# Opening stage of a two-layer decoder trunk: remainders moved from GpSimd to VectorE, and to an accumulating DMA for the last three steps

## The chip, the cores and the metric

One core of one Trainium2 chip runs the kernel. The metric is the device time of one execution in microseconds (us); less is better. Before the change the median of three runs is 1287.88 us (1286.55 to 1293.02).

## What is computed

Two layers over 512 rows of 1024 channels (`x`), conditioned on one vector `c`:

```python
c_act = silu(c)
for l in range(2):
    sh1, sc1, g1, sh2, sc2, g2 = split(c_act @ w_ada[l] + b_ada[l], 6)
    h = rmsnorm(x, norm1_w[l]) * (1 + sc1) + sh1
    x = x + g1 * hybrid_mixer(h, cos, sin, w_in[l], ...)     # attention and state-space heads
    h = rmsnorm(x, norm2_w[l]) * (1 + sc2) + sh2
    x = x + g2 * swiglu(h, w_gate_up[l], w_down[l])
```

`cos` and `sin` are of `positions * inv_freq`. What matters here is the very beginning of layer 0: the norm of `x`, the two modulation vectors `sc1` and `sh1`, the hidden `h`, and the first 808 columns of `h @ w_in[0]`.

## The kernel before, in words

Every f32 product is done as three matmuls in a rounded type (fp32r): an operand is split into a high part (`hi`, `hh`: the rounded copy, made on ScalarE) and a remainder (`lo`, `hl`: the operand minus its high part). The product is hi·hh + hi·hl + lo·hh (`mm3`, line 316; `mmrow`, line 321). So each weight tile costs a DMA, a cast on ScalarE and a subtraction on VectorE or GpSimd.

The stage that changes is the block at lines 1088 to 1156, called the opening below. In the trace it ends where the first `wps` matmul begins, which belongs to the next stage.

- `xin` is loaded transposed into `xT` (channels on partitions), in two halves of the rows, four DMAs each (line 231). `cb` is `c` on all partitions; `silu` is applied to it.
- `stat` (line 1102) makes the squares on ScalarE, adds them up on VectorE, and sums them over the channels by matmuls with `ones`. `scale` (line 1111) turns the sum into the row scale `rs0`, with a logarithm and an exponential on ScalarE and three operations on VectorE.
- Then come eight steps, k = 0 to 7, one for each 128 channels. `load(k)` (line 1114) fetches two tiles of `w_ada` (`raws`, 512 KB each; one for `sc1`, tile 8 + k, one for `sh1`, tile k) and one slab of `w_in` (`rawk`, 404 KB). A tile of `w_ada` is multiplied by `cb` and summed on VectorE (`ada1`, line 332, the result goes into `mods`); `ada_fin` (line 347) adds the bias, and makes `gn` = (1 + sc1) · norm weight. `slab` (line 295) casts `rawk` to `hik` on ScalarE and subtracts to get `lok` on GpSimd (line 300).
- `hid` (line 422) makes the hidden of those 128 channels: `ht` on VectorE (needs `gn`), `hh` on ScalarE (adds `sh1`), a second ScalarE pass `hu`, and `hl` = `hu` - `hh` on GpSimd (line 433).
- `mms` (line 1120) issues the step's 21 matmuls: 12 with 424 columns and 9 with 512.
- In step 2 (`PLAN['STK']`) the small tables are made (`small_tables`, line 252): 25 small VectorE operations on 64 columns for the rotary angles (`ang`, `kk`, `kh`, `kl`), three sines on ScalarE with a table load before them and another after them, and casts of the mask on GpSimd.

All loads go through one queue (SP), in program order. The order of the other engines is set by a scheduler at build time, except where `kept` or `pinned` holds the written order (lines 1129 to 1141). `warm` issues matmuls on `ones` that compute nothing. Buffers that tie the steps together: six for `raws`, three each for the slab and for its high part and remainder.

Of the kernel before, what the change touches and what calls it, by code (L numbers as in the profile page):

```python
# [8 lines left out]
F32 = mybir.dt.float32  # L9
# [3 lines left out]
AF = mybir.ActivationFunctionType  # L13
# [58 lines left out]
    'KHV': 0,  # L72
# [3 lines left out]
P = 128  # L76
S = 512
# [68 lines left out]
class Kept:  # L146
    """an engine; while kept, its instructions stay in the order they are written in"""
# [19 lines left out]
class Stream:  # L167
    """steps for the tensor engine; a step yields the time from which on the next should find its data"""
# [26 lines left out]
def trunk(ctx, tc, xin, cin, pos, eye, consts, small, wada, ws, out):  # L195
# [39 lines left out]
    tc.keep_in_program_order(nc.scalar.preload_act_table_set("silu_and_others"))  # L235
    nc.sync.dma_start(cb, cin.partition_broadcast(P))
    xload(HALVES[0])
    xload(HALVES[1])
    nc.sync.dma_start(sm[0], small[0])
# [12 lines left out]
    def small_tables():  # L252
        ve.tensor_copy(idb, ident)
        mk = kc[:, K_MASK:K_MASK + P]
        for i in range(4):
            tc.keep_in_program_order(ge.tensor_copy(mkb[:, i, :], mk))
# [3 lines left out]
        ang, kk, kh, kl = (tiny(nm, n, 1) for nm in ("ang", "kk", "kh", "kl"))  # L260
# [19 lines left out]
        ve.tensor_scalar(ang, ang, pi, -pi, op0=ALU.min, op1=ALU.max)  # L280
        v4 = lambda t: t.rearrange("p (c f) -> p c f", f=16)
# [3 lines left out]
        ve.tensor_copy(cs2[:, :, 1, :], cs2[:, :, 0, :])  # L285

# [8 lines left out]
    def slab(raw, src, name, n, eng=None):  # L295
        r2, hi, lo = (t.rearrange("p a b -> p (a b)")[:, 0:n] for t in (
            raw, wp.tile([P, 8, P], F32R, name=f"hi{name}", tag="hi"), wp.tile([P, 8, P], F32R, name=f"lo{name}", tag="lo")))
        nc.sync.dma_start(r2, src[:, 0:n])
        se.copy(hi, r2)
        (eng or ve).tensor_tensor(lo, r2, hi.bitcast(F32), op=ALU.subtract)  # L300
        return hi, lo
# [19 lines left out]
    def mmrow(ps, h, w, k, c):  # L321
        """one k of the latents of chunk c, rows on the partitions"""
# [46 lines left out]
    def rsqrt(y, x, scale, name, a=None, out=None):  # L369
        """y = (x * scale + EPS) ** -0.5: exp(-ln / 2) and a Newton step"""  # L370
# [13 lines left out]
    class Norm:  # L384
        """adaLN over the columns of xT: squares added up tile by tile, then the row scale and the hidden"""
# [16 lines left out]
        def scale(self, sl, ps=None, rb=None):  # L402
            """(mean square + eps) ** -0.5 of the rows in sl, on all partitions"""
# [55 lines left out]
    def mixer(l, h, rows, first):  # L459
        s_ = sm[l]  # L460
        with tc.tile_pool(name=f"mx{l}", bufs=1) as mp:
# [14 lines left out]
            def decays():  # L476
                """time steps and decays, [step in chunk, (chunk, head)]"""
# [40 lines left out]
            def dense():  # L518
                """the rest of W_in, then the first half of the rows of W_out, tile by tile"""
# [56 lines left out]
            with tc.tile_pool(name=f"up{l}", bufs=2) as up, psum(f"u{l}", mm=2, ms=2, at=4):  # L576
# [3 lines left out]
                # latents, a chunk's rows on the partitions (their row scale follows after the up-projections)  # L580
# [33 lines left out]
                # rotary factors with the norm weights in them  # L614
# [7 lines left out]
                def rope(x, cw, sw, shape, name, re=ve):  # L622
                    """in place on x[..., 32]"""
# [109 lines left out]
            with tc.tile_pool(name=f"s2{l}", bufs=2) as sp, psum(f"v{l}", ms=2, sc=2, pt=1, op=1, mm=2):  # L733
# [12 lines left out]
                # attention over (chunk, heads), in three steps  # L746
# [34 lines left out]
                def values(c, h0, g):  # L781
                    """two heads at a time, one in each half of the columns of the array: channels on the partitions"""
# [39 lines left out]
                def norms():  # L822
                    """one over the sums of the probabilities, turned to where the channels are; then the products' split"""
# [19 lines left out]
                # the state space part, chunk by chunk  # L843
# [148 lines left out]
    def out_proj(l, mix, nrm, sl, kept):  # L992
        """one half of the rows; the weight tiles that lie on chip at its end are kept for the other half"""
# [93 lines left out]
    for l in range(L):  # L1087
        if l == 0:
            with tc.tile_pool(name="s0", bufs=6) as s0, psum("s", ms=1, st=NCH + NC0):
# [12 lines left out]
                def stat(sl):  # L1102
                    sq = s0.tile([P, KT, S // 2], F32, name=f"sq01{sl.start}", tag="sq", bufs=2)
                    for k in range(0, KT, 2):
                        se.activation(sq[:, k:k + 2], xT[:, k:k + 2, sl], AF.Square)
                        if k > 0:
                            ve.tensor_tensor(sq[:, 0:2], sq[:, 0:2], sq[:, k:k + 2], op=ALU.add)
                    for j in range(2):
                        te.matmul((nst if sl.start else sps[-2])[:, 0:S // 2], ones, sq[:, j], start=j == 0, stop=j == 1)
# [3 lines left out]

                def load(k):
                    for t in (8 + k, k):
                        ada1(0, t, s0.tile([P, 8, P], F32, name=f"raws{t}", tag="raws"))
                        ada_fin(0, t, t + 1)
                    return slab(wraw(f"k{k}"), wk0[k], f"k{k}", NS0, ge)
# [11 lines left out]
                te.pinned = True  # L1130
                warm(PLAN['WU'])
                se.activation(cb, cb, AF.Silu)
                stat(HALVES[0])
                exp_ln_tables()
                warm(PLAN['WV'])
                scale(HALVES[0])
                stat(HALVES[1])
                scale(HALVES[1])
                warm(PLAN['WW'])
                te.pinned = False  # L1140
                ve.kept = se.kept = False
# [151 lines left out]
```

## Time and profile before

| | |
|---|---|
| median of three runs | 1287.88 us |
| lowest, highest run | 1286.55, 1293.02 us |
| span of the profiled execution | 1284.9 us |
| PE busy | 1211.4 us (94%) |
| VectorE (DVE) busy | 634.1 us (49%) |
| ScalarE (ACT) busy | 519.9 us (40%) |
| GpSimd (POOL) busy | 531.1 us (41%) |
| DMA moved | 162.34 MB |

The profiled execution is known by its span alone, from its first instruction to its last; no separate time is listed for it. PE is the matmul engine, PEld its weight loads, SP the DMA queue. Times in rows are us from the start of the span. "Busy" of an instruction runs from its start to its end, so an instruction that is held up by another engine looks long.

### The profile page before, as it was taken

The numbers are of one execution on the slowest core, as the hardware profiler recorded it, in microseconds if no ns is written. First come the engines' busy times: TensorE is split into PE (matmuls) and PEld (weight loads), VectorE is DVE, ScalarE is ACT, GpSimd is POOL, SyncE is SP. The second block draws the span as 40 slices with busy tenths as digits, with TensorE's granted clock in tenths as the row PEclk, the third lists the DMA queues.
The fourth block names the chain that finished last, engine by engine and source line by source line (L and its number), as shares of the span: only waits on it lengthen the run. The fifth ranks groups of instructions, "written<-read, shape, count | busy, mean of one in ns | idle before, by whom it ended". The sixth has DMA issues, their size and how long they took to land. (4 is left out here: it accounts for less than half of the span.)

```text
span 1284.9 us, 16463 instructions
## 1 busy us (share of the span) xinstructions
PE 1211.4 (94%) x6343; PEld 1005.1 (78%) x6344; DVE 634.1 (49%) x1128; ACT 519.9 (40%) x896; POOL 531.1 (41%) x310
## 2 busy tenths in 40 slices
PE   6889796889999999999998999979999999999998
PEld 6768674689888888888887887659988888888888
DVE  6979778879245545211128885576821111110100
ACT  4366774435322222222226668654532222222110
POOL 2651145263676666523333232346333333333231
PEclk9899898899999999999999899999999999999999
DMA  9433352464477777423223222103333332323331
GB/s 321 154 125 102 114 164 99 150 200 143 129 241 238 239 240 237 134 87 97 96 71 107 83 79 70 34 33 91 124 115 99 90 106 84 102 94 107 115 101 40
DMA packets 47855, 162.34 MB, mean 126 GB/s; under 512 B 5344, under 2 KB 8224, under 8 KB 47776
## 3 DMA queue, kind: packets, MB, share of 16 engines
q1 hardware_dynamic: 47776, 161.29, 38.8%
q8 instruction: 50, 0.82, 0.3%
q14 instruction: 29, 0.24, 0.1%
HBM read 159.14 MB, written 2.13 MB: 126 GB/s over the span
## 5 line engine op out<-in xcount | busy, mean ns | idle before, releaser
L292 POOL TENSOR_TENSOR lo<-raw,hi 128x1024 fp32r<-128x1024 f32 x108 | 272.6, 2524 | 338.6 <-ACT hi L156 338.5
L156 ACT CAST hi<-raw 128x1024 fp32r<-128x1024 f32 x179 | 188.0, 1051 | 500.8 <-issue 183.5
L140 PE MATMUL gup<-hl,hi 128*128 128x512 f32 (+1 forms) x736 | 280.4, 381 | 0.0
L140 PE MATMUL gup<-hh,lo 128*128 128x512 f32 (+1 forms) x736 | 279.9, 381 | 0.0
L140 PE MATMUL gup<-hh,hi 128*128 128x512 f32 (+1 forms) x736 | 278.6, 381 | 0.0
L156 DVE TENSOR_TENSOR lo<-raw,hi 128x1024 fp32r<-128x1024 f32 x71 | 88.9, 1253 | 152.6 <-ACT hi L156 150.8
L140 PEld LDWEIGHTS gup<-hh,lo 128*128 128x128 f32 x736 | 139.1, 189 | 26.5
L140 PEld LDWEIGHTS gup<-hl,hi 128*128 128x128 f32 x736 | 139.0, 189 | 26.0 <-DVE hl L156 0.2
L140 PEld LDWEIGHTS gup<-hh,hi 128*128 128x128 f32 x736 | 138.4, 189 | 26.2
L156 DVE SCALAR_TENSOR_TENSOR rawa<-rawa,cb 128x1024 f32<-128x1024 f32 x77 | 111.0, 1443 | 76.7 <-DMA rawa<-wada 76.5
L140 PE MATMUL dps<-ah,hi 128*128 128x512 f32 x308 | 121.8, 396 | 0.0
L140 PE MATMUL dps<-al,hi 128*128 128x512 f32 x308 | 121.8, 396 | 0.0
L140 PE MATMUL dps<-ah,lo 128*128 128x512 f32 x308 | 121.8, 396 | 0.0
L156 DVE TENSOR_TENSOR sg<-sg,gup 128x512 f32<-128x512 f32 x44 | 30.3, 688 | 179.6 <-PE gup L140 173.5
L440 POOL TENSOR_TENSOR al<-sg,ah 128x512 fp32r<-128x512 f32 x44 | 67.6, 1535 | 97.2 <-ACT ah L156 93.6
L140 PE MATMUL ops<-hh,hi 128*128 128x256 f32 x256 | 74.4, 290 | 3.1 <-ACT hi L156 1.5
L140 PE MATMUL ops<-hl,hi 128*128 128x256 f32 x256 | 72.5, 283 | 1.0 <-POOL hl L440 1.0
L140 PE MATMUL wps<-hh,hi 128*128 128x512 f32 x168 | 70.8, 422 | 2.4 <-DVE xbc L156 2.4
L140 PE MATMUL ops<-hh,lo 128*128 128x256 f32 x256 | 72.5, 283 | 0.3 <-POOL lo L292 0.3
L140 PEld LDWEIGHTS dps<-al,hi 128*128 128x128 f32 x308 | 57.9, 188 | 14.1
L140 PEld LDWEIGHTS dps<-ah,hi 128*128 128x128 f32 x308 | 57.9, 188 | 14.0
L140 PEld LDWEIGHTS dps<-ah,lo 128*128 128x128 f32 x308 | 57.9, 188 | 13.9
(303 smaller groups left out, 2103.3 us busy)
## 6 DMA issues: line engine op xcount, KB each, us to landing
raw<-ws SPq DMA_DIRECT2D x181, 512.0 KB, 3.5
rawa<-wada SPq DMA_DIRECT2D x80, 512.0 KB, 4.4
raws<-wada SPq DMA_DIRECT2D x16, 512.0 KB, 5.3
ar<-ard SPq DMA_DIRECT2D x8, 512.0 KB, 3.9
rawk<-ws SPq DMA_DIRECT2D x8, 404.0 KB, 5.4
xT<-xin SPq DMA_DIRECT2D x8, 256.0 KB, 5.9
out<-xT SPq DMA_DIRECT2D x7, 256.0 KB, 2.6
rawr<-ws SPq DMA_DIRECT2D x4, 424.0 KB, 3.2
```

The source lines that it names most:

```text
L140: self._put(self.tc.nc.tensor.matmul(out, lhsT, rhs, **kw), 4 * n if rhs.dtype == F32 else n)
L156: i = f(*args, **kw)
L292: (eng or ve).tensor_tensor(lo[:, :n], raw[:, :n], hi[:, :n].bitcast(F32), op=ALU.subtract)
L440: (eng or ve).tensor_tensor(lo, src, hi.bitcast(F32), op=ALU.subtract)
```

## The change

Ten lines of the plan and of comments aside, the diff does this:

- Two small loads (`posi`, and the frequencies of `kc`) go first on the SP queue, then the first half of `x`, `cb`, `sm`, the second half. The rest of `kc` and `eye` are loaded in step 1.
- The rotary angles are computed at the very start, the sines between the squares and the statistics.
- The squares are no longer added on VectorE: PE sums all eight tiles of a half. Two of the four squares of the second half are made on VectorE.
- The bias and the `1 +` of `gn` are folded into one vector `gb` beforehand, so that `gn` takes one operation.
- `hl` is made on VectorE from `ht`, `sh1` and `hh` in one operation; `hu` is gone.
- `lok` is made on VectorE for k = 0 to 4. For k = 5 to 7 ScalarE writes minus the high part into `lok`, and a DMA issued from GpSimd adds the weights to it from memory.
- Step 0 issues its matmuls by halves of the rows; the second group of warming matmuls stands after both scales, the third is gone.

```diff
     tc.keep_in_program_order(nc.scalar.preload_act_table_set("silu_and_others"))
+    nc.sync.dma_start(posi, pos)
+    nc.sync.dma_start(kc[:, K_FREQ:NK], consts[:, K_FREQ:NK])
+    xload(HALVES[0])
     nc.sync.dma_start(cb, cin.partition_broadcast(P))
-    xload(HALVES[0])
+    nc.sync.dma_start(sm[0], small[0])
     xload(HALVES[1])
-    nc.sync.dma_start(sm[0], small[0])
...
         nc.sync.dma_start(r2, src[:, 0:n])
         se.copy(hi, r2)
+        if eng == "dma":
+            se.activation(lo, r2, AF.Identity, scale=-1.0)
+            ge.dma_start(lo, src[:, 0:n], accum_op=ALU.add)
+            return hi, lo
         (eng or ve).tensor_tensor(lo, r2, hi.bitcast(F32), op=ALU.subtract)
...
-                def stat(sl):
+                def squares(sl):
                     sq = s0.tile([P, KT, S // 2], F32, name=f"sq01{sl.start}", tag="sq", bufs=2)
                     for k in range(0, KT, 2):
-                        se.activation(sq[:, k:k + 2], xT[:, k:k + 2, sl], AF.Square)
-                        if k > 0:
-                            ve.tensor_tensor(sq[:, 0:2], sq[:, 0:2], sq[:, k:k + 2], op=ALU.add)
-                    for j in range(2):
-                        te.matmul((nst if sl.start else sps[-2])[:, 0:S // 2], ones, sq[:, j], start=j == 0, stop=j == 1)
+                        x = xT[:, k:k + 2, sl]
+                        if sl.start and k > 2:
+                            ve.tensor_tensor(sq[:, k:k + 2], x, x, op=ALU.mult)
+                        else:
+                            se.activation(sq[:, k:k + 2], x, AF.Square)
+                    return sq
+
+                def stat(sl, sq):
+                    for k in range(KT):
+                        te.matmul((nst if sl.start else sps[-2])[:, 0:S // 2], ones, sq[:, k], start=k == 0, stop=k == KT - 1)
...
+                nw1 = sm[0][:, C_N1:C_N1 + 8]
+                gb = s0.tile([P, 8], F32, name="gb", bufs=1)
                 def load(k):
                     for t in (8 + k, k):
                         ada1(0, t, s0.tile([P, 8, P], F32, name=f"raws{t}", tag="raws"))
-                        ada_fin(0, t, t + 1)
-                    return slab(wraw(f"k{k}"), wk0[k], f"k{k}", NS0, ge)
+                        m = mods[0][:, t:t + 1]
+                        if t < 8:
+                            ve.tensor_tensor(m, m, sm[0][:, C_BADA + t:C_BADA + t + 1], op=ALU.add)
+                        else:
+                            ve.scalar_tensor_tensor(gn[0][:, k:k + 1], m, nw1[:, k:k + 1], gb[:, k:k + 1], op0=ALU.mult, op1=ALU.add)
+                    return slab(wraw(f"k{k}"), wk0[k], f"k{k}", NS0, "dma" if k > 4 else None)
...
+                angles()
                 warm(PLAN['WU'])
+                sq = squares(HALVES[0])
                 se.activation(cb, cb, AF.Silu)
-                stat(HALVES[0])
+                stat(HALVES[0], sq)
+                sq = squares(HALVES[1])
+                sines()
                 exp_ln_tables()
+                ve.scalar_tensor_tensor(gb, sm[0][:, C_BADA + 8:C_BADA + 16], 1.0, nw1, op0=ALU.add, op1=ALU.mult)
+                stat(HALVES[1], sq)
+                scale(HALVES[0])
+                scale(HALVES[1])
                 warm(PLAN['WV'])
-                scale(HALVES[0])
-                stat(HALVES[1])
-                scale(HALVES[1])
-                warm(PLAN['WW'])
...
                     if k == 1:
+                        nc.sync.dma_start(kc[:, 0:K_FREQ], consts[:, 0:K_FREQ])
                         nc.sync.dma_start(ki, eye)
-                        nc.sync.dma_start(posi, pos)
-                        nc.sync.dma_start(kc, consts)
                     w = load(k)
                     for sl in HALVES if k == 0 else (FULL,):
-                        last = hid(0, 1, h, k, rs0[:, sl], sl, ge)
-                    for sl in HALVES if k < PLAN['KHV'] else (FULL,):
+                        last = hid(0, 1, h, k, rs0[:, sl], sl)
                         mms(k, w, sl)
                     if k == PLAN['STK']:
                         with tc.issue_after(last.ins):
-                            small_tables()
-                        exp_ln_tables()
+                            ve.tensor_copy(idb, ident)
+                            se.copy(cs2[:, :, 1, :], cs2[:, :, 0, :])
+                            for i in range(4):
+                                tc.keep_in_program_order(ge.tensor_copy(mkb[:, i, :], kc[:, K_MASK:K_MASK + P]))
```

`angles()` and `sines()` are the two halves of `small_tables` with the same operations; `ang` and `kh` become tiles that live through the kernel.

## Rows read from the trace of the kernel before

**Rows 1.** Busy time by stretch: us, PE, PEld, DVE, ACT, POOL, clock, DMA share, GB/s.

```profile
200.00:645.00 445.00, 423.58 (x2160) 352.12 (x2160) 219.47 (x336) 149.62 (x222) 226.02 (x117) 0.98 0.51 167
```

**Rows 2.** Timeline of PE: start us, us, operation; the opening's first matmul, step 4's and 5's, the next stage's.

```profile
21.78 0.44 PE L140 MATMUL st<-hik,hh 128*128 128x424 f32 x1
...
55.19 0.35 PE L140 MATMUL st<-hik,hh 128*128 128x424 f32 x1
...
59.62 0.36 PE L140 MATMUL st<-hik,hh 128*128 128x424 f32 x1
...
77.64 0.40 PE L140 MATMUL wps<-hh,hi 128*128 128x512 f32 x1
```

**Rows 3.** PE's waits in the opening: us in total, times, longest us.

```profile
PE st L140 <- POOL hl L433: 7.0, 6, 2.0
```

**Rows 4.** Busy time by stretch, from VectorE's first `raws` to its last `mods`.

```profile
14.99:70.57 55.58, 44.31 (x192) 36.62 (x192) 54.25 (x96) 20.11 (x31) 32.58 (x24) 0.88 0.59 207
```

**Rows 5.** Timeline of VectorE: one `ht` of step 1, then steps 5 and 6, then the last.

```profile
28.13 0.74 DVE L156 SCALAR_TENSOR_TENSOR ht<-xT,gn,rs 128x512 f32<-128x512 f32 x1
...
53.18 1.63 DVE L156 SCALAR_TENSOR_TENSOR ht<-xT,gn,rs 128x512 f32<-128x512 f32 x1
54.73 2.94 DVE L156 SCALAR_TENSOR_TENSOR raws<-raws,cb 128x1024 f32<-128x1024 f32 x1
...
59.53 1.63 DVE L156 SCALAR_TENSOR_TENSOR ht<-xT,gn,rs 128x512 f32<-128x512 f32 x1
...
70.41 0.16 DVE L156 TENSOR_TENSOR mods<-mods,sm 128x1 f32<-128x1 f32 x1
```

**Rows 6.** Timeline of GpSimd over the same steps, and its last `hl`.

```profile
52.98 1.28 POOL L433 TENSOR_TENSOR hl<-hu,hh 128x512 fp32r<-128x512 f32 x1 [1.46 <-ACT hu L156]
54.22 2.37 POOL L300 TENSOR_TENSOR lok<-rawk,hik 128x808 fp32r<-128x808 f32 x1
...
72.02 1.26 POOL L433 TENSOR_TENSOR hl<-hu,hh 128x512 fp32r<-128x512 f32 x1 [2.73 <-ACT hu L156]
```

**Rows 7.** VectorE by line and form, 14.9 to 70.6 us: busy us, mean ns, idle before.

```profile
L156 DVE SCALAR_TENSOR_TENSOR raws<-raws,cb 128x1024 f32<-128x1024 f32 x16 | 26.4, 1650 | 0.0
L156 DVE TENSOR_TENSOR mods<-mods,sm 128x1 f32<-128x1 f32 x16 | 9.5, 594 | 0.2
L156 DVE SCALAR_TENSOR_TENSOR ht<-xT,gn,rs 128x512 f32<-128x512 f32 x7 | 9.1, 1295 | 0.3
L156 DVE SCALAR_TENSOR_TENSOR ang<-kl,ang 128x64 f32<-128x64 f32 x4 | 1.9, 481 | 0.0
L156 DVE SCALAR_TENSOR_TENSOR ang<-kk,ang 128x64 f32<-128x64 f32 x3 | 1.8, 586 | 0.1
...
L156 DVE SCALAR_TENSOR_TENSOR ang<-kh,ang 128x64 f32<-128x64 f32 x4 | 0.9, 218 | 0.1
```

**Rows 8.** Single tiles on VectorE: duration ns min/median/max, first and last start us, forms.

```profile
L156 DVE SCALAR_TENSOR_TENSOR raws<-raws,cb x16: 1210/1218/2974, 15.0 to 67.4; 128x1024 f32<-128x1024 f32 x16
...
L156 DVE TENSOR_TENSOR mods<-mods,sm x16: 145/160/1884, 16.7 to 70.4; 128x1 f32<-128x1 f32 x16
...
L156 DVE TENSOR_TENSOR lo<-raw,hi x71: 1174/1225/2306, 121.8 to 1260.0; 128x1024 fp32r<-128x1024 f32 x71
...
L156 DVE SCALAR_TENSOR_TENSOR hl<-ht,mods,hh x48: 473/482/2609, 292.0 to 928.7; 128x256 fp32r<-128x256 f32 x48
```

**Rows 9.** GpSimd by line and form, 14.9 to 74 us: busy us, mean ns.

```profile
L292 POOL TENSOR_TENSOR lo<-raw,hi 128x1024 fp32r<-128x1024 f32 x1 | 2.4, 2398 | 0.0
...
L619 POOL TENSOR_TENSOR sq<-sn,sm 128x128 f32<-128x128 f32 x1 | 0.4, 411 | 0.0
```

**Rows 10.** The slabs' loads (tile `rawk`, eight of 404 KB), from issue to landing.

```profile
DMA to landing us min/median/max: 3.1/5.4/8.5
```

**Rows 11.** Timeline of ScalarE: the table load before the sines, and step 5's cast.

```profile
37.39 1.28 ACT L156 ACT_TABLE_LOAD   x1
...
52.81 0.85 ACT L156 CAST hik<-rawk 128x808 fp32r<-128x808 f32 x1
```

More of the change, by code (lines that the diff above doesn't have):

```diff
@@ L71 @@
     'WV': 14,
-    'KHV': 0,
     'STK': 2,
@@ L250, in exp_ln_tables, with angles @@
         tc.keep_in_program_order(nc.scalar.preload_act_table_set("natural_log_exp_and_others"))
[L252 to L256, printed above, removed]
+    ang, kh = (cp.tile([P, NCH * 16], F32, name=n) for n in ("ang", "kh"))
+    def angles():
         n = NCH * 16
@@ L259, in small_tables @@
         ve.tensor_copy(pf, posi)
-        ang, kk, kh, kl = (tiny(nm, n, 1) for nm in ("ang", "kk", "kh", "kl"))
+        kk, kl = (tiny(nm, n, 1) for nm in ("kk", "kl"))
         ve.tensor_tensor(ang.rearrange("p (c f) -> p c f", f=16), pf.unsqueeze(2).broadcast_to([P, NCH, 16]),
@@ L280, in small_tables, with sines @@
         ve.tensor_scalar(ang, ang, pi, -pi, op0=ALU.min, op1=ALU.max)
+    def sines():
         v4 = lambda t: t.rearrange("p (c f) -> p c f", f=16)
@@ L284, in small_tables @@
         se.activation(cs2[:, :, 0, :], v4(ang), AF.Sin)
-        ve.tensor_copy(cs2[:, :, 1, :], cs2[:, :, 0, :])
     def wsplit(raw, name, n, eng=None):
@@ L1130, in trunk @@
                 te.pinned = True
+                angles()
                 warm(PLAN['WU'])
+                sq = squares(HALVES[0])
                 se.activation(cb, cb, AF.Silu)
-                stat(HALVES[0])
+                stat(HALVES[0], sq)
+                sq = squares(HALVES[1])
+                sines()
                 exp_ln_tables()
+                ve.scalar_tensor_tensor(gb, sm[0][:, C_BADA + 8:C_BADA + 16], 1.0, nw1, op0=ALU.add, op1=ALU.mult)
+                stat(HALVES[1], sq)
+                scale(HALVES[0])
+                scale(HALVES[1])
                 warm(PLAN['WV'])
-                scale(HALVES[0])
-                stat(HALVES[1])
-                scale(HALVES[1])
-                warm(PLAN['WW'])
-                te.pinned = False
-                ve.kept = se.kept = False
+                te.pinned = ve.kept = se.kept = False
                 for k in range(KT):
                     if k == 1:
+                        nc.sync.dma_start(kc[:, 0:K_FREQ], consts[:, 0:K_FREQ])
                         nc.sync.dma_start(ki, eye)
-                        nc.sync.dma_start(posi, pos)
-                        nc.sync.dma_start(kc, consts)
                     w = load(k)
                     for sl in HALVES if k == 0 else (FULL,):
-                        last = hid(0, 1, h, k, rs0[:, sl], sl, ge)
-                    for sl in HALVES if k < PLAN['KHV'] else (FULL,):
+                        last = hid(0, 1, h, k, rs0[:, sl], sl)
                         mms(k, w, sl)
```

## The prediction

> **What bounds the kernel now.** I first read the busy time by stretch. In the long middle stretch PE is busy 423.6 of 445 us [rows 1], so most of the kernel is paced by its matmuls and does not change. The diff touches only the opening, so I read that next. PE's timeline shows the first matmul of the eight steps at 21.78 us and the first one of the next stage at 77.64 us [rows 2]. One step that does not wait, step 4, goes from 55.19 to 59.62: 4.43 us. Eight of them would take 35.4 us, and the opening takes 55.9. So some 20 us of it are waits, and the list of waits puts the largest share on `hl`, made by GpSimd [rows 3].
>
> GpSimd is not what is short, though. From VectorE's first `raws` (14.99) to its last `mods` (70.41 + 0.16 = 70.57) VectorE is busy 54.25 of 55.58 us, GpSimd 32.58 and PE 44.31 [rows 4]. VectorE paces the opening: `ht` of step 5 starts at 53.18, that of step 6 at 59.53, a period of 6.35 us [rows 5], against PE's 4.43.
>
> The next thing to see is why it is so busy. `ht` takes 0.74 us in step 1 and 1.63 in step 5; `raws` takes 1.22 at the median and 2.94 at 54.73 [rows 5, 8]. Beside it GpSimd runs `hl` from 52.98 to 54.26 and `lok` from 54.22 to 56.59 [rows 6]. 54.26 + 0.55 is the end of `ht`; 56.59 + 1.02 is the end of `raws`. VectorE's operations with two operands in SBUF stand still while GpSimd works on SBUF, and are done after. So about a third of VectorE's time in the opening is standing still.
>
> **The change, part by part.** I add up VectorE's chain from 14.99 on, since it sets the opening's end.
>
> Standing still, removed with `lok` and `hl` on GpSimd: busy time of a group minus its count times its unhindered duration [rows 7, 8]. `raws` 26.4 - 16 x 1.218 = 6.9; `mods` 9.5 - 16 x 0.160 = 6.9; `ht` 9.1 - 7 x 0.74 = 3.9; the two hindered kinds of `ang` 1.9 - 4 x 0.22 = 1.0 and 1.8 - 3 x 0.22 = 1.1. Sum **-19.8**.
>
> The angles, moved ahead: 25 operations of 0.2 (218 ns each for the unhindered kind, a little of it overlapped): **-5.0**. Ahead of 14.99 VectorE waits for data in any case, and the two small loads that they need go first on SP's queue. On that queue they, and `sm`, push back `x` by three issues, while `cb` gets out of the way of half of it; the bytes ahead of the first `raws` stay the same but for these few, so I count nothing there. The squares' additions go and two products of squares come, both nearly all ahead of 14.99: nothing. Summing squares on PE adds matmuls where PE has only warming ones: nothing, and if that cover is gone it delays the second scale.
>
> `gn` in one operation instead of two, eight times: 8 x 0.16 = **-1.3** [rows 8].
>
> Added: `hl` on VectorE, 7 x 0.74 (the 512-wide `ht`, also three inputs) + 2 x 0.48 (the 256-wide `hl` elsewhere) = **+6.1** [rows 5, 8]. `lok` of steps 0 to 4: 1.174 x 808 / 1024 = 0.93, five times: **+4.7** [rows 8]. The first half's row scale, three 256-wide operations that were done before 14.99, now comes after the sines, a table load of 1.28 before them if the loaded set lacks the sine, and one after [rows 11]: 3 x 0.48 = **+1.4**, while the logarithm is hidden by the two `raws` products that need no scale. GpSimd still does four rotary tables of 0.41 and may start `lo` of the next stage's two tiles (2.4 each) under the last steps [rows 9]: between 0 and 6.4; as most of that came after the last VectorE work before, I take **+2.0**.
>
> Chain: 55.58 - 26.1 + 14.2 = 43.7, from 14.99 to 58.7, with the last `hl` in it. Before, the last `hl` ended at 72.02 + 1.26 = 73.28 [rows 6]. Behind it come the same matmuls. **Gain 14.6.**
>
> The accumulating DMA: no row of the trace has a DMA from GpSimd, or one that adds. Step 5's cast stood 59.62 - 52.81 = 6.8 us ahead of its first matmul [rows 2, 11]; with steps of about 4.7 instead of 6.35 that is 5.0. The cast and the negated copy take 0.85 each, so 3.3 us are left for it. From below, a landing time of 3.1 (the quickest slab): nothing late. From above, 17 (twice the slowest slab, 8.5, since it reads the destination too) [rows 10]. I take the median slab, 5.4: it is the same number of bytes from the same memory. That is 2.1 late; PE waits 0.7 for `hh` and 0.74 for `hl` at that point in any case, so **0.6** shows. Behind this DMA on GpSimd stand only `lo` of the next stage's tiles; behind the negated copy on ScalarE stands the next step's `hh`, 0.85 later in three steps, which ScalarE (20.11 busy of 55.58 [rows 4]) has room for, `hu` (0.7 a step) being gone; behind `hl` on VectorE stand the next `raws`, and PE waits for it (a rival below). By the Trainium skill (DMA: Bandwidth & Descriptors, section on the anatomy of one DMA on the GpSimd path) a plain one costs about 2.0 us and its bytes over 436 GB/s; an estimate for 414 kB by that page is 2.9 us, nothing would be late, and the sum would be 0.6 better; no run here shows it yet.
>
> From 77.64 on nothing is changed but the clock time, and the weights that it needs come through the same queue, whose buffers are free earlier. Sum: 14.6 - 0.6 = **14.0 us**. The profiled span, 1284.9, would become 1270.9; the median of the runs is 3.0 above that span, so I predict 1287.9 - 14.0 = **1273.9, say 1274**.
>
> **The rivals.**
>
> *PE becomes the bound* (0.20). If VectorE also starts earlier than 14.99 (its first `raws` did not wait, so it had landed before) and nothing of GpSimd hinders it, the first matmul comes at about 18 (earlier than 21.78 by the two stalls and the late scale) and the end at 18 + 35.4 + 1.5 = 55: gain 22.7, **1265**. For: the sum leaves VectorE 4.6 a step in the last three, PE's own 4.43. Against: five steps still carry `lok`.
>
> *VectorE waits for ScalarE* (0.14). `hl` on VectorE needs `hh`, which needs `mods`, two places earlier in VectorE's own queue. Where the scheduler puts nothing between, VectorE idles 0.95 (0.73 of `hh` and two hand-overs) a step: 7.6 us, **1280**, reading 14.6 - 7.6 = 7 with little late. For: before, GpSimd took that wait off VectorE. Against: the next step's `raws` needs nothing and stood right behind `mods`.
>
> *The accumulating DMA paces the last steps, mildly* (0.07). With 8.5 us each, one after the other: the first is issued at about 46.5 (end at 63.6, three steps of 4.6, a lead of 5.0, two casts), the third lands at 46.5 + 25.5 = 72, the rest of the step takes 4.2: 76.2 against 77.64, **1286**.
>
> *The same, but slower than before* (0.05). It decides from (77.64 - 4.2 - 46.5) / 3 = 9.0 us each. At 17 the third lands at 97.5 and the opening ends at 101.7: 24 later, **1312**. For: adding means reading the destination, and VectorE, now busy with two-operand work, may hold up GpSimd's part of the DMA, as GpSimd held up VectorE before [rows 5, 6]. Against: three slabs only, loaded well ahead. The Trainium skill (SBUF — State Buffer, the section on SBUF's two separate sides) warns of that: descriptors of a GpSimd DMA wait while VectorE holds the shared port in a two-port mode, and it names 3.1 us instead of 0.62 for one DMA; an estimate by that page is 2.5 us more for each, and no run here shows it yet.
>
> *The change does not reach the end* (0.04): the next stage waits for its own weights until 77.6 in any case. **1288**. Against: those were held up by buffers that are freed earlier.
>
> **How the numbers follow.** The forecast itself has 0.50. A difference of 0.5%, 6.4 us, is about what a measurement of this kernel can tell from no change; faster means 1281.4 or less. Faster: 0.50 + 0.20 + 0.11 of the waiting case = 0.81. Same: 0.03 of it, 0.07 and 0.04 = 0.14. Slower: 0.05. The range goes from the PE-bound case, 1265 less 1, to the waiting case with what is open of the DMA, 1283: it leaves out the last three cases, 0.16.
>
> **What would show it.** Right: `raws` on VectorE near 1.22 in every step, no POOL row in steps 0 to 7 but tables, a period of 5 to 5.5 us in steps 1 to 4 and about 4.6 after, the first `wps` at about 64. Wrong: `raws` or `ht` still at twice their length; idle VectorE before `hl`; PE waiting for `lok` in steps 5 to 7; or the first `wps` early and a new wait right behind it. The forecast fails if the GpSimd DMAs land later than 9 us after their issue, or if the first scale comes so late that VectorE runs dry before step 0.

## The result and the profile after

The changed kernel takes 1275.18 us (median of 4 runs, 1271.27 to 1278.04) where the kernel before takes 1288.12 beside it: a ratio of 0.9892, 95% interval 0.9867 to 0.9918, or 12.9 us less. Timed again with the last experiments it took 1274.67 against 1286.99: 0.9905, 0.9878 to 0.9932. The forecast was 1274. The sum was right to about 1 us; the mechanism behind its last part was not, and that is what this text is about. The runs behind these two medians spread from 1271 to 1279 us, so versions that differ by 2 or 3 us below are not told apart by their times.

| us | before | after | after, second profile |
|---|---|---|---|
| span of the profiled execution | 1284.9 | 1274.1 | 1272.0 |
| first matmul of the eight steps | 21.8 | 22.4 | 22.9 |
| first `wps` (the eight steps are over) | 77.6 | 64.9 | 64.0 |
| `wps` goes on with its second tile | 85.7 | 73.0 | 72.1 |
| first `kvps` | 94.2 | 80.0 | 80.8 |
| first `ops<-hh` (layer 0's out-projection) | 244.0 | 230.1 | 231.5 |
| first `gup` (layer 0's MLP) | 306.3 | 295.6 | 294.9 |

Read it downwards. The opening gives 12.7 and 13.6 us, 13.9 and 12.5 of them reach the out-projection, 10.7 and 11.4 the MLP, 10.8 and 12.9 the end.

First the busy time from VectorE's first `raws` to its last `mods`, the stretch that answers to [rows 4] (columns as there):

```profile
16.07:52.86 36.79, 30.31 (x153) 26.94 (x152) 36.79 (x77) 14.65 (x21) 5.24 (x8) 0.93 0.97 333
```

VectorE needs 36.8 us where the stretch took 55.6, without a gap, and GpSimd is busy 5.2 us instead of 32.6. VectorE by form over this stretch (busy us, mean ns, idle before), against [rows 7]:

```profile
L155 DVE SCALAR_TENSOR_TENSOR raws<-raws,cb 128x1024 f32<-128x1024 f32 x16 | 19.4, 1211 | 0.0
L155 DVE SCALAR_TENSOR_TENSOR ht<-xT,gn,rs 128x512 f32<-128x512 f32 x7 | 5.1, 735 | 0.0
L155 DVE TENSOR_TENSOR lok<-rawk,hik 128x808 fp32r<-128x808 f32 x5 | 4.9, 986 | 0.0
L155 DVE SCALAR_TENSOR_TENSOR hl<-ht,mods,hh 128x512 fp32r<-128x512 f32 x6 | 4.4, 737 | 0.0
L155 DVE SCALAR_TENSOR_TENSOR gn<-mods,sm,gb 128x1 f32<-128x1 f32 x8 | 1.6, 204 | 0.0
```

`raws` takes 1211 ns on average instead of 1650, `ht` 735 instead of 1295: in this stretch next to nothing stands still any more. But VectorE is done long before the steps are: its last `mods` ends at 52.86, the steps at 64.89. PE's timeline (start us, us, operation, idle before it and its releaser):

```profile
22.43 0.65 PE L139 MATMUL st<-hik,hh 128*128 128x424 f32 x2 [3.27 <-ACT hh L155]
...
33.20 0.94 PE L139 MATMUL st<-hik,hh 128*128 128x424 f32 x4
...
37.60 0.93 PE L139 MATMUL st<-hik,hh 128*128 128x424 f32 x4
...
42.22 1.03 PE L139 MATMUL st<-hik,hh 128*128 128x424 f32 x4
...
50.80 0.46 PE L139 MATMUL st<-lok,hh 128*128 128x424 f32 x1 [3.16 <-DMA lok<-ws]
...
64.89 0.40 PE L139 MATMUL wps<-hh,hi 128*128 128x512 f32 x1
...
72.99 0.47 PE L139 MATMUL wps<-hh,hi 128*128 128x512 f32 x1 [2.45 <-DVE xbc L155]
```

From its first matmul to the first `wps` the timeline lists one wait of PE, 3.16 us, for the accumulating DMA. The rows at 33.20, 37.60 and 42.22 begin steps 2, 3 and 4; a step that waits for nothing takes 4.40 us. And PE's clock falls; the busy time by stretch (granted clock third from the end):

```profile
22.00:26.00 4.00, 3.57 (x14) 3.13 (x15) 4.00 (x9) 1.54 (x3) 0.00 (x0) 0.74 1.03 413
26.00:30.00 4.00, 4.00 (x23) 3.89 (x23) 4.00 (x8) 1.48 (x2) 0.00 (x0) 0.84 1.03 410
...
50.00:54.00 4.00, 3.20 (x10) 2.97 (x11) 2.86 (x8) 1.33 (x2) 0.85 (x1) 0.65 1.01 252
54.00:58.00 4.00, 4.00 (x20) 3.58 (x19) 0.18 (x1) 1.68 (x2) 0.76 (x1) 0.92 0.76 167
```

Each fall came behind idle time: before 22.43 PE had waited 3.27 us, before 50.80 3.16 us, and then a part of its matmuls ran at the lower level, 1.2 GHz. Idle time did not always bring a fall: in the second profile the clock stayed at 1.00 behind a wait of 2.33 us for the same DMA. An estimate of the work not done is 4 x (0.26 + 0.16) = 1.7 us behind the first wait and 4 x (0.35 + 0.08) = 1.7 behind the second.

The first of these cost nothing at the end, since VectorE still set the pace there. PE's step 4 began at 42.22, as soon as its `hh` was made (ScalarE's timeline; 41.44 + 0.72 = 42.16):

```profile
41.44 0.72 ACT L155 ACTIVATE hh<-ht,mods 128x512 fp32r<-128x512 f32 x1 [3.25 <-DVE ht L155]
```

Up to there VectorE needs 4.7 to 4.9 us a step, from `ht` to `ht`, against PE's 4.40. That is 19.79 us behind the first matmul. The version below with the last three remainders on GpSimd does the same up to step 4, and its two profiles have 19.80 with the clock at 0.75 and 0.83 between 22 and 30 us, and 19.79 at 1.00 throughout. Only a lower clock there is felt: 0.50 and 0.65 in the second profile of the changed kernel made it 20.41. From step 5 on, where the DMA makes `lok`, VectorE needs 3.8 us a step, and PE sets the pace: 42.22 + 4 x 4.40 + 3.16 + 1.7 = 64.7, and the trace has 64.89.

GpSimd's timeline has the three new DMAs and then nothing until the next stage's remainders; the list of DMA issues has the time to landing (last number, median):

```profile
44.02 1.01 POOL L303 DMA_DIRECT2D lok<-ws  x1 [23.84 <-ACT lok L155]
47.83 0.87 POOL L303 DMA_DIRECT2D lok<-ws  x1 [2.79 <-ACT lok L155]
51.62 0.85 POOL L303 DMA_DIRECT2D lok<-ws  x1 [2.93 <-ACT lok L155]
57.24 2.39 POOL L293 TENSOR_TENSOR lo<-raw,hi 128x1024 fp32r<-128x1024 f32 x1 [4.76 <-ACT hi L155]
```

```profile
lok<-ws POOLq DMA_DIRECT2D x3, 404.0 KB, 6.7
```

Step 5's went out at 44.02 and let PE go at 50.80; the three landed within 6.7 to 7.0 us. VectorE's timeline shows both ends of its chain:

```profile
13.14 1.51 DVE L155 TENSOR_TENSOR sq<-xT 128x512 f32<-128x512 f32 x2 [4.42 <-DMA xT<-xin]
...
16.07 1.25 DVE L155 SCALAR_TENSOR_TENSOR raws<-raws,cb 128x1024 f32<-128x1024 f32 x1
...
52.72 0.14 DVE L155 TENSOR_TENSOR mods<-mods,sm 128x1 f32<-128x1 f32 x1
57.81 2.37 DVE L155 SCALAR_TENSOR_TENSOR hl<-ht,mods,hh 128x512 fp32r<-128x512 f32 x1 [4.96 <-ACT hh L155]
```

At the start VectorE stood 4.42 us for the last slices of `x` with the first `raws` queued behind its squares, so that `raws` began 1.1 us later than before. At the end the last `hl` waited 4.96 us for `hh`. ScalarE's timeline says why:

```profile
56.11 1.05 ACT L155 CAST hi<-raw 128x1024 fp32r<-128x1024 f32 x1 [4.78 <-issue]
57.06 0.72 ACT L155 ACTIVATE hh<-ht,mods 128x512 fp32r<-128x512 f32 x1
```

A cast for the next stage stood ahead of `hh` in ScalarE's queue. The profile names no releaser for it; it began at 56.11, as PE went from step 5 to step 6 (56.09; in the second profile 54.72 and 54.70), so it seems to have been late because PE was. PE did not notice: it ran steps 6 and 7 from 56.1 to 64.89 without a listed wait, itself late by the DMA. It came close, for that `hl` ended at 60.18 and was used from 60.67 on.

### The profile page after: what moved, and what is told of

The parts are those of the page before. It is cut to its first block, busy times and chain, and to the rows that moved or that the text cites. A ratio compares the mean times of both kernels' runs of the same rounds, so it can differ in the third digit from the quotient of the medians.

```text
span 1274.1 us, 16423 instructions
## 1 busy us (share of the span) xinstructions
PE 1206.0 (95%) x6340; PEld 1004.2 (79%) x6341; DVE 622.2 (49%) x1130; ACT 513.1 (40%) x887; POOL 504.2 (40%) x296
## 5 line engine op out<-in xcount | busy, mean ns | idle before, releaser
L155 DVE SCALAR_TENSOR_TENSOR rawa<-rawa,cb 128x1024 f32<-128x1024 f32 x77 | 108.3, 1407 | 77.7 <-DMA rawa<-wada 77.7
L139 PE MATMUL wps<-hh,hi 128*128 128x512 f32 x168 | 70.1, 418 | 2.4 <-DVE xbc L155 2.4
L139 PEld LDWEIGHTS dps<-ah,lo 128*128 128x128 f32 x308 | 57.9, 188 | 13.9
L139 PEld LDWEIGHTS dps<-al,hi 128*128 128x128 f32 x308 | 57.9, 188 | 13.9
```

Source lines behind the costliest of these rows:

```text
L139: self._put(self.tc.nc.tensor.matmul(out, lhsT, rhs, **kw), 4 * n if rhs.dtype == F32 else n)
L155: i = f(*args, **kw)
```

## The experiments

All edits are of the changed kernel. The opening's checkpoints of every run (us; "last `mods`" is VectorE's last one in the eight steps):

| kernel | last `mods` | first `wps` | second tile | first `kvps` | first `gup` | time, median (runs) |
|---|---|---|---|---|---|---|
| before | 70.4 | 77.6 | 85.7 | 94.2 | 306.3 | 1288.1 (4) |
| after | 52.7 | 64.9 | 73.0 | 80.0 | 295.6 | 1275.2 (4) |
| after again | 53.2 | 64.0 | 72.1 | 80.8 | 294.9 | 1274.7 (6) |
| old engines | 67.2 | 73.4 | 82.6 | 91.2 | 304.2 | 1283.4 (10) |
| all on VectorE | 57.2 | 63.4 | 71.4 | 80.0 | 294.9 | 1272.3 (4) |
| last three on GpSimd | 60.1 | 67.6 | 74.3 | 81.3 | 293.2 | 1269.0 (1) |
| the same, again | 60.5 | 68.1 | 74.8 | 81.8 | 294.5 | 1272.5 (6) |
| plain DMA | 52.8 | 62.0 | 70.1 | 77.1 | 287.8 | 1266.8 (1) |
| `hl` on GpSimd | 56.5 | 63.7 | 75.8 | 84.3 | 297.2 | 1276.5 (1) |
| angles late | 54.9 | 63.8 | 76.1 | 84.4 | 297.2 | 1273.2 (1) |
| load ahead | 52.1 | 63.4 | 71.7 | 78.7 | 290.5 | 1272.0 (5) |
| the same, again | 53.1 | 64.2 | 72.5 | 79.5 | 294.5 | 1276.3 (6) |
| all and next on VectorE | 55.2 | 61.4 | 72.5 | 81.3 | 296.9 | 1276.2 (6) |
| ahead, all on VectorE | 53.8 | 64.4 | 72.7 | 79.7 | 292.6 | 1275.2 (6) |

**The old engines under the new start.** All eight remainders and every `hl` go back to GpSimd; the rearranged start and the folded `gn` stay.

```diff
-return slab(wraw(f"k{k}"), wk0[k], f"k{k}", NS0, "dma" if k > 4 else None)
+return slab(wraw(f"k{k}"), wk0[k], f"k{k}", NS0, ge)
...
-last = hid(0, 1, h, k, rs0[:, sl], sl)
+last = hid(0, 1, h, k, rs0[:, sl], sl, ge)
```

> The changed kernel with all remainders (slab and hidden) on GpSimd as before: the rearranged opening alone. Theory A (the gain is VectorE's standing still, 19.8 us less, against 10.8 of work taken over): raws and ht are stretched again to a mean of 1.5 us or more, the period is again near 6, and only the angles (5) and the folded bias (1.3) are gained: next stage at 71 to 74, the whole about 1283. Theory B (the rearrangement of the start carries most of the 12.75): next stage at 68 or earlier, the whole about 1278 or less.

The ratio to the kernel before was 0.9976 (0.9953 to 1.0), and checkpoint and time lie where theory A had them. VectorE by form in this kernel:

```profile
L155 DVE SCALAR_TENSOR_TENSOR raws<-raws,cb 128x1024 f32<-128x1024 f32 x16 | 29.4, 1839 | 0.0
L155 DVE SCALAR_TENSOR_TENSOR ht<-xT,gn,rs 128x512 f32<-128x512 f32 x7 | 12.2, 1741 | 0.8
```

`raws` is back at 1839 ns, `ht` at 1741. VectorE's last `mods` comes 14.5 us later than in the changed kernel, although `lok` and `hl`, 10.2 us of work ahead of it there, are not VectorE's here. So the rearranged start alone is worth 4.2 us at the first `wps`, and the move off GpSimd 8.5 more. It is this kernel against the changed one that shows the stretching to be what the change removes.

**No DMA: all eight remainders on VectorE.**

```diff
-return slab(wraw(f"k{k}"), wk0[k], f"k{k}", NS0, "dma" if k > 4 else None)
+return slab(wraw(f"k{k}"), wk0[k], f"k{k}", NS0)
```

> The changed kernel with the remainder of the slab on VectorE in all eight steps (no accumulating DMA). In the changed kernel PE waits 3.2 us for the first DMA-made remainder and runs at half clock for some 3.5 us behind it, and the next stage's first matmul is at 64.89. Theory A (the DMA costs more than it saves): the wait and the slow stretch go, VectorE gets 3 x 0.93 = 2.8 us more, its last hl comes at about 56.5, and the next stage begins at 60 to 61.5, 3.5 to 5 earlier; the whole about 1271. Theory B (VectorE paces the opening, the DMA is worth its VectorE time): the next stage begins 2 to 3 later, at 67 to 68, the whole about 1278.

The ratio was 0.9888 (0.9844 to 0.9933), with the changed kernel's inside it. PE's wait for `lok` was gone, but the first `wps` came only 1.5 us earlier, which neither the wait's 3.16 nor theory A's 3.5 to 5 is, and the first `kvps` at the same time. Timelines of VectorE, GpSimd and PE in this kernel:

```profile
54.12 3.20 DVE L155 TENSOR_TENSOR lok<-rawk,hik 128x808 fp32r<-128x808 f32 x1
```

```profile
53.66 2.80 POOL L293 TENSOR_TENSOR lo<-raw,hi 128x1024 fp32r<-128x1024 f32 x1 [33.22 <-ACT hi L155]
```

```profile
58.86 1.03 PE L139 MATMUL st<-hik,hh 128*128 128x424 f32 x4 [2.26 <-ACT hh L155]
```

VectorE's last `lok` met GpSimd's `lo` of the next stage and took 3.20 us instead of 0.99; `mods`, `ht` and `hh` came later by that, and PE waited 2.26. One wait had taken the place of the other. GpSimd's operation was stretched too, to 2.80 us from 2.4.

**The last three remainders on GpSimd**, as a subtraction, in place of the DMA (`ge if k > 4 else None`), twice:

> The changed kernel with the remainder of steps 5 to 7 on GpSimd, as before the change, in place of the DMA. Theory A (GpSimd's subtraction makes VectorE stand still): three operations of 1.9 to 2.4 us on GpSimd, raws or ht beside them stretched by 1 to 1.8 each, 3 to 5 us more VectorE time than the changed kernel up to its last mods (52.86), so 56 to 58; no wait of PE for a DMA; next stage at 61 to 64. Theory B (moving work off VectorE is free wherever it goes): VectorE's last mods stays within 0.7 of 52.9, next stage at 58 to 60.5.

> The last three remainders by GpSimd's subtraction in place of the DMA, timed again after one single time of 1268.95. Theory A (the middle of the kernel varies by some us from one order of instructions to the next, and the opening is what the edit sets: first kvps 81.3 against 80.0): 1272 to 1279, within 0.3% of the changed kernel. Theory B (GpSimd is the better place for these three): 1266 to 1271, faster than the changed kernel by over 0.3%.

VectorE's timeline beside one of the three, and that one on GpSimd's, show the stretching even on an operation of one element to a partition:

```profile
54.36 1.89 DVE L155 SCALAR_TENSOR_TENSOR gn<-mods,sm,gb 128x1 f32<-128x1 f32 x1
...
57.31 2.87 DVE L155 SCALAR_TENSOR_TENSOR ht<-xT,gn,rs 128x512 f32<-128x512 f32 x1
```

```profile
54.22 2.01 POOL L305 TENSOR_TENSOR lok<-rawk,hik 128x808 fp32r<-128x808 f32 x1 [3.48 <-ACT hik L155]
```

GpSimd's `lok` ran from 54.22 to 56.23 and its next `lo` from 56.20 to 59.63. VectorE's last `mods` came 7.4 us later than in the changed kernel, the first `wps` 2.7 later, the first `kvps` 1.3 later: more than the first theory's 56 to 58 and 61 to 64, which had not counted the next stage's `lo` on the last `ht`. The end was not later at all: the single time of 1268.95 became a median of 1272.5 (0.9881, 0.9854 to 0.9908) beside 1274.67 for the changed kernel. The second theory's 1266 to 1271 was missed; the two can't be told apart.

**The DMA without the addition.** It overwrites the negated weights, so the low part of steps 5 to 7 is the whole weight.

```diff
-ge.dma_start(lo, src[:, 0:n], accum_op=ALU.add)
+ge.dma_start(lo, src[:, 0:n])
```

> The changed kernel with the GpSimd DMAs writing the weights into the remainder without adding (the remainder of the last three slabs is then the weights themselves: this part of the computation is changed). Theory A (the 6.7 us from issue to landing is the full memory queue and the size, as for the slabs' own loads of 6.4): landing 5.5 to 7, PE's wait for the remainder 2.5 to 3.7. Theory B (adding is what is slow, since the destination is read too): landing 4.5 or less, PE's wait below 1.

The tile `lok` of this kernel, landing times in us, least, median and most:

```profile
DMA to landing us min/median/max: 4.4/4.8/5.3
```

Against 6.7 to 7.0 with the addition: adding costs 1.9 us a transfer, and the issue on GpSimd takes 0.53 us instead of 0.87 (medians). PE's wait shrank from 3.16 to 1.22, and the first `wps` came at 62.0. The clock behind the shorter wait stayed at 1.00, as it did behind the 2.33 of the second profile of the changed kernel. Theory A's landing time was too long by at least 0.7, theory B's too short by a little. The slabs' own loads of the same size, on SP's queue, took 6.3 in this kernel and 6.4 in the changed one (medians). The single time, 1266.8, and the first `gup` are the earliest of all; 2.9 us of that come out of the opening, and they are kept at the second tile and at the first `kvps`. The stages up to `gup` were 4.9 us shorter still in this one execution. 2.3 of that lie between the out-projection and `gup`, where the second profile of the changed kernel is shorter by 2.1 too; in both the clock stood at 1.00 from 250 to 290 us (see below for the first profile). Why the other 2.6, behind the first `kvps`, were gained was not followed up.

**`hl` back on GpSimd alone**, `lok` as in the changed kernel:

```diff
-last = hid(0, 1, h, k, rs0[:, sl], sl)
+last = hid(0, 1, h, k, rs0[:, sl], sl, ge)
```

> The changed kernel with hl on GpSimd from hu, as before the change; the slab remainders as in the changed kernel. Theory A (standing still beside a GpSimd subtraction costs VectorE as much as doing it itself): VectorE loses 6.1 us of hl and gains 0.9 or more of standing still in each of eight steps, its last mods stays within 2 of 52.9, hl comes 1.2 later in each step because of hu and the slower subtraction, next stage 0 to 4 later than 64.9. Theory B (VectorE's load alone counts): its last mods 4 to 6 earlier, next stage at 63 or earlier.

**The angles back into step 2**, with the sines and the second table load there, as before:

```diff
-                angles()
...
-                sines()
...
                     if k == PLAN['STK']:
                         with tc.issue_after(last.ins):
...
+                            angles()
+                            sines()
...
+                        exp_ln_tables()
```

> The changed kernel with the rotary angles and the sines back in step 2 and their table loads with them. Theory A (VectorE has no room in the steps, and the 25 operations cost their own 5 us there): next stage 3.5 to 6 later than 64.9, at 68.5 to 71. Theory B (after the change VectorE has room, PE and the DMA pace the opening): within 1.5 of 64.9.

In both VectorE is later in the eight steps (its last `mods` by 3.8 and 2.2 us), and in both the first `wps` is not later. For the angles that is theory B. For `hl` it is neither: `mods` came later than theory A's 2 us, the first `wps`, 1.2 earlier, later than theory B's 63. With `hl` on GpSimd PE waited for it four times, 2.2 us in all, but for the DMA only 0.32 instead of 3.16, and its clock was back at 1.00 from 30 us on. With the angles in the steps PE waited for `hh` in steps 2 to 4 (PE's timeline):

```profile
32.37 1.04 PE L139 MATMUL st<-hik,hh 128*128 128x424 f32 x4 [0.77 <-ACT hh L155]
...
37.64 1.07 PE L139 MATMUL st<-hik,hh 128*128 128x424 f32 x4 [0.61 <-ACT hh L155]
...
43.31 1.04 PE L139 MATMUL st<-hik,hh 128*128 128x424 f32 x4 [0.96 <-ACT hh L155]
...
76.08 0.77 PE L139 MATMUL wps<-hh,hi 128*128 128x512 f32 x1 [6.68 <-DVE xbc L155]
```

That is 2.3 us, and 0.3 more for one `hl`, for angles that had been counted as 5.0 on VectorE. Step 4 began 1.1 us later than in the changed kernel. Behind it this execution got more than that back: PE waited 1.56 for the DMA instead of 3.16, and the granted clock was 1.00 from 22 to 62 us, where the changed kernel lost some 1.7 us behind its wait. So neither kernel shows that VectorE had room in the steps; they show that its lateness took the place of the wait for the DMA. What both kernels lose comes behind the opening. The second tile of `wps` waits 6.4 and 6.7 us for `xbc` instead of 2.4, since VectorE there empties its last bank of the opening's sums only after an `ul` and a `lo` of the next stage (from 74.89 and 75.20, the changed kernel from 71.45). The first `kvps` is 4.3 and 4.4 later. That order was the scheduler's; it was not forced back by an experiment.

**The next step's weights ahead of this step's hidden**, so that the DMA has a longer lead, twice:

```diff
+ws_ = {0: load(0)}
 for k in range(KT):
...
-    w = load(k)
+    w = ws_.pop(k)
+    if k + 1 < KT:
+        ws_[k + 1] = load(k + 1)
```

> The changed kernel with step k+1's loads, casts and remainders written ahead of step k's hidden, so that the negated copy and the adding DMA of steps 5 to 7 can be issued a step earlier. Theory A (the DMA is late because its copy stands one step ahead at most): ScalarE makes the negated copy of step 5 before 40, PE's wait for the remainder falls from 3.2 to below 1, the half-clock stretch behind it goes, next stage at 60.5 to 62.5, the whole about 1272. Theory B (the order is set by when data and buffers come, not by where it is written): the copy stays within 1.5 of 42.8, the wait within 1 of 3.2, next stage at 64 to 66.

> The weights of step k+1 prepared ahead of the hidden of step k, timed again after a median of 1272.04. Theory A (what the opening gains is given back behind it): 1272 to 1278, within 0.3% of the changed kernel. Theory B (the DMA's lead was what the changed kernel lacks, 1.5 us at the first kvps and 5 at the first gup): 1267 to 1272.

PE's timeline of the first profile:

```profile
24.83 1.07 PE L139 MATMUL st<-hik,hh 128*128 128x424 f32 x2 [5.72 <-ACT hh L155]
...
54.84 0.46 PE L139 MATMUL st<-lok,hh 128*128 128x424 f32 x1 [0.67 <-DMA lok<-ws]
```

The wait for the DMA fell from 3.16 to 0.67, and step 0 began 2.4 us later, because step 1's work on VectorE now stands ahead of step 0's hidden. Step 5's DMA, issued at 42.32 and so 1.7 us earlier, was not waited for any more, but PE was later by then too (step 5 from 49.23, in the changed kernel from 46.71). The 0.67 is for the next one, which landed 8.1 us after its issue at 46.74. The negated copy came at 41.12 and the first `wps` at 63.4, between the two theories. The first median, 1272.04, was not found again: 1276.29 in the second session (0.9908, 0.9882 to 0.9934). Two profiles of this one kernel differ by 4.0 us at the first `gup`.

**All remainders on VectorE, the next stage's two `lo` too**, to take away what stretched the last `lok`:

```diff
-return slab(wraw(f"k{k}"), wk0[k], f"k{k}", NS0, "dma" if k > 4 else None)
+return slab(wraw(f"k{k}"), wk0[k], f"k{k}", NS0)
...
-mtile(0, B_IN + 4 + t, h, f"wps0{t}", eng=ge)
+mtile(0, B_IN + 4 + t, h, f"wps0{t}")
```

> All slab remainders on VectorE (no accumulating DMA), and the remainders of the next stage's first two weight tiles on VectorE too, so that GpSimd subtracts nothing in the opening or right behind it. With the slabs alone moved, VectorE's last lok took 3.20 us instead of 0.99, because GpSimd made the next stage's remainder beside it, PE waited 2.3 us for the hh behind it, and the next stage began at 63.4. Theory A (that one GpSimd subtraction is what holds the last step): the last lok takes 1.0 us, the wait goes, the next stage begins at 60.8 to 61.8; what VectorE gets on top (two of 1.2 us) costs less than 1.5 after that; the whole 1269 to 1272. Theory B (the last step is late for another reason): the next stage begins at 63 or later, the whole 1272 or more.

VectorE's, ScalarE's and PE's timelines:

```profile
54.30 0.99 DVE L155 TENSOR_TENSOR lok<-rawk,hik 128x808 fp32r<-128x808 f32 x1
```

```profile
56.05 0.72 ACT L155 ACTIVATE hh<-ht,mods 128x512 fp32r<-128x512 f32 x1 [2.29 <-DVE ht L155]
```

```profile
22.86 1.07 PE L139 MATMUL st<-hik,hh 128*128 128x424 f32 x2 [3.28 <-ACT hh L155]
...
52.10 1.04 PE L139 MATMUL st<-hik,hh 128*128 128x424 f32 x4
...
56.82 1.07 PE L139 MATMUL st<-hik,hh 128*128 128x424 f32 x4
...
61.35 0.40 PE L139 MATMUL wps<-hh,hi 128*128 128x512 f32 x1
...
72.52 0.76 PE L139 MATMUL wps<-hh,hi 128*128 128x512 f32 x1 [5.54 <-DVE xbc L155]
```

Every `lok` takes 0.99 us, and PE has no listed wait from 22.86 to the first `wps` at 61.35. It is VectorE that sets the pace here to the end: the last `hh` is made at 56.77, and PE's last step begins at 56.82, 4.72 us after the one before. So the 38.5 us are not PE's alone, whose eight steps of 4.40 would be 35.2. The start at half clock (0.50 and 0.68 in the first two stretches of 4 us) was made up for by then. Theory A was right so far, and wrong on what follows: all but 0.5 us is given back where the second tile of `wps` goes on, at 72.5, after waiting 5.54 us for VectorE. Part of that wait is once more the scheduler's order: a `ul` and a `lo` (from 68.86 and 70.44, some 2.1 us) stand ahead of the last bank, at 71.64, as in the two kernels above. The time is 1276.2 (0.9924, 0.9895 to 0.9952).

**Both: ahead, and all on VectorE**, beside the changed kernel once more:

> Weights prepared a step ahead, and all eight remainders on VectorE, without the accumulating DMA. Theory A (the DMA is worth nothing net, VectorE's chain has room for three more remainders of 0.99, and PE paces the steps): no wait of PE for lok, first wps 61 to 64, first kvps 78 to 81, total within 0.3% of the changed kernel. Theory B (with the lead given, the DMA does spare VectorE what the end needs): first wps 65 or later, kvps 81 or later, total slower than the one with load ahead by 2 to 4 us.

> The changed kernel once more, beside three others on one chip. Both theories: 1272 to 1278 us, ratio to the kernel before 0.987 to 0.992. It is the measure for the other three.

Without the DMA PE waited 0.33 us behind its late first matmul (25.15), and the first `wps` came at 64.4, the first `kvps` at 79.7. The time, 1275.2 (0.9905, 0.9881 to 0.9929), is that of the changed kernel, and not 2 to 4 us over the one with the load ahead. The first `wps` was a little beyond theory A's 61 to 64. So the DMA is worth nothing that these runs can tell: what it spares VectorE, 3.8 us a step instead of 4.73, PE loses again by waiting for it.

No version beats the changed kernel: the four timed together lie between 1272.5 and 1276.3, with intervals that all overlap.

## Why the prediction was right, and where it was not

**What bounded the kernel** was read rightly: VectorE, held up by GpSimd. The old engines under the new start bring the stretching back, and 8.5 us with it. One reading went too far: "some 20 us of it are waits". PE's waits from 21 to 78 us in the kernel before are the 7.0 of [rows 3] and these for `hh`:

```profile
PE st L140 <- ACT hh L156: 4.8, 3, 3.1
```

That is 11.8. Most of the rest is half clock, some 6 us by the clock and PE's busy time between 30 and 38 and between 46 and 58. Two of these stretches:

```profile
34.00:38.00 4.00, 4.00 (x12) 3.45 (x12) 3.86 (x12) 1.95 (x3) 0.55 (x1) 0.50 0.40 117
...
50.00:54.00 4.00, 4.00 (x12) 3.49 (x12) 3.82 (x6) 2.09 (x3) 2.54 (x2) 0.50 0.63 205
```

The sum does not use the 20, but the clock, 0.88 already in [rows 4], went unread.

**The chain on VectorE** was forecast at 43.7 us with the last `hl`; up to the last `mods` it took 36.8, so 6.2 less than the same stretch of the forecast. The terms that the rows carried held: `raws` and `ht` unhindered, `hl` 5.3 + 0.7 for 6.1, `lok` 4.9 for 4.7. Five things were missing. The squares' additions had not all been ahead of 14.99 (0.8 us of them lay behind it). 1.3 us of [rows 4] had been idle. The angles' 25 operations had taken 8.7 us of VectorE, 1.6 more than the 1.0, 1.1 and 5.0 subtracted. Of the first half's row scale only 0.9 us, not 1.4, lay behind the first `raws`. And the **+2.0 for GpSimd's residual** did not occur ahead of the last `mods`: its only clear stretch was on the last `hl` (2.37 for 0.74), where nobody waited. 0.8 + 1.3 + 1.6 + 0.5 + 2.0 = 6.2.

**Step that failed: "Behind it come the same matmuls."** The last `hl` was to set the end, with 4.4 us behind it. VectorE set the pace up to step 4 only; from step 5 on it was out of the way, and PE, its wait for the DMA and its clock behind that wait set the end. VectorE's last `mods` could come 3.8 and 2.2 us later without a later first `wps`, since the wait for the DMA shrank and the clock stayed up behind it. So the rival "PE becomes the bound" had the right engine for the last three steps, and missed its price in four places. The first matmul came not at 18 but at 22.43, since VectorE did not start earlier: `raws` stood behind squares that waited 4.42 us for `x`. That they would have run at once otherwise was not tried. Up to step 4 PE went at VectorE's 4.7 to 4.9 us a step (2.1 us in all). Then came the DMA's 3.2 us, where forecast and rival had 0.6 and nothing, and 1.7 us of half clock behind it, which neither had. 1265 became 1275.

**Mis-sized: the accumulating DMA.** Its landing was taken as 5.4 us from the loads of the same size [rows 10]; it was 6.7. The slabs' loads themselves were at 6.4 in the changed kernel, so [rows 10] was no measure for the opening after the change. The lead was 5.6 us (cast at 42.07, PE ready at 47.64), near the 5.0 of the forecast; two casts of 1.63, 0.3 to the issue and 6.7 make 3.1 late, and 3.16 show, not 0.6. The cover that was named for the difference, PE's own waits for `hh` and `hl` at that point, had gone with VectorE's lateness: a wait that is counted as cover has to be there still after the change. The plain DMA took 4.8 us. By the Trainium skill (DMA: Bandwidth & Descriptors, the anatomy of one DMA on the GpSimd path) that would be 2.9, an estimate by that page; neither the plain nor the adding transfer agrees here. Both write a tile of the rounded type from f32 weights, and beside the loads on SP's queue; whether either makes the plain one longer was not tried. The slower rival, from 9.0 us a transfer on, stayed 2 us away.

**VectorE waiting for `hh`** did not happen in steps 1 to 6: the scheduler put a `raws` between. It happened at the last step, 4.96 us, behind a ScalarE cast of the next stage, and was hidden.

**Behind the opening** "nothing is changed" held to within 2 to 3 us. In the first profile 3.2 us went in layer 0's out-projection, in the second 1.1. Part of the difference is clock (some 1.4 us, an estimate from busy time and clock), as the same stretch of both profiles shows, first the first, then the second:

```profile
270.00:280.00 10.00, 8.38 (x53) 7.92 (x53) 7.06 (x13) 4.76 (x9) 1.40 (x2) 0.83 0.63 207
```

```profile
270.00:280.00 10.00, 8.37 (x66) 7.92 (x65) 7.34 (x14) 4.55 (x9) 1.96 (x2) 1.00 0.66 209
```

PE is busy 8.4 us of the ten in both, at 0.83 and at 1.00 of its clock. Why it fell in one execution of the same program and not in the other stays open.

**So the total was right by errors that cancelled**, which is luck. With nothing for the DMA the forecast had the first `wps` at 58.7 + 4.4 = 63.1. Without the wait and the clock behind it the trace would have had 42.22 + 4 x 4.40 = 59.8, an estimate: 3.3 us earlier, by the shorter chain. The DMA's wait and 1.7 us of half clock put 4.9 on that, where 0.6 had been counted: 4.3 us later.

## What to carry to other kernels

Where an engine is busy all the time, look at the shortest duration of each of its operations before believing that it has that much work; here a third was standing still beside GpSimd, and the cure was to use GpSimd less. When the bound moves to another engine, go through the sum again from that engine's side: the covers counted on the old path are gone, and the gain stops at the new bound. Where two engines are within a tenth of each other, as VectorE's 4.73 us a step and PE's 4.40 are here, see who follows whom at each step: a wait too short for the list, or a slower clock that is made up for, does not show in a sum. And follow a gain to the next place where the old bound works: the eight steps could be made 3.5 us shorter still, and 3.0 of that were waited away 11 us later, where VectorE empties the sums. The order of its queue decides that: the plain DMA's 2.9 us were kept there.

## What the runs showed that was not expected

- A DMA that adds took 6.7 us to land where the same one without adding took 4.8, and 0.87 us of GpSimd's time to issue instead of 0.53.
- Standing still strikes small operations as hard as big ones: `gn`, one element to a partition, took 1.89 us beside GpSimd's subtraction instead of 0.20. The Trainium skill (SBUF — State Buffer, SBUF: two separate sides) has one engine blocked for the whole of the other's instruction, where VectorE's operation takes two inputs from SBUF and GpSimd reads SBUF; this row agrees: `gn` ended at 56.25, GpSimd's `lok` at 56.23. It goes the other way too: the `lo` that GpSimd began at 56.20, beside a `raws` from 56.17, took 3.43 us instead of 2.4.
- The sine needed no table load of its own behind the squares, where 1.28 had been reckoned with. ScalarE's timeline of the changed kernel has the sines, and only then a load, the one ahead of the logarithm:

```profile
12.93 0.39 ACT L155 ACTIVATE sn<-kh 128x64 f32<-128x64 f32 x2
13.22 0.24 ACT L155 ACTIVATE cs<-ang 128x64 f32<-128x64 f32 x1
13.48 1.28 ACT L251 ACT_TABLE_LOAD   x1
```

- The opening's clock is not the same from run to run of one program: 0.74 and 0.50 between 22 and 26 us in the two profiles of the changed kernel, 0.75 and 1.00 in the two with the last three remainders on GpSimd. The first `wps` differs by 0.9 and 0.5 us between them, and is not the earlier one where the clock was higher.
